# One decoder step in fp32 on one core: the RWKV stage in units of one chunk and eight heads, with two attention stages moved ahead of it

## The chip, the cores and the metric

The kernel runs on one core of a Trainium2 chip. The metric is the device time of one execution in microseconds; the time of a kernel is the median of its runs. TensorE (PE, with its weight loads PEld), VectorE (DVE), ScalarE (ACT), GpSimd (POOL) and SyncE (SP, which issues most of the DMAs) each work through their own instructions in the order in which the program was written out, and wait for each other by semaphores.

## What is computed

One layer over 1024 prompt tokens and 8 sample tokens, d_model 2048, all in fp32. `p = rmsnorm(x) @ w_in` gives the inputs of four branches of width 512 and a gate for each; the gated branches are joined and go through `w_out`. Cut to what matters here:

```python
A  o = softmax-difference attention (4 heads; the samples also over 512 paged cache rows)
B  for each token t, 8 heads of 64:          # RWKV-7, the stage that is changed
     sa = S @ a_t;  S = S * w_t + sa b_t^T + v_t k_t^T;  y_t = S @ r_t
C  Mamba-2 scan (chunks of 128)
X  cross-attention into 256 memory rows (the samples into a cache of their own)
x  = x + concat(A * silu(dg), B * silu(rg), C-branch with its gate mz, X * silu(xg)) @ w_out
```

## The kernel before, in words

**The large products.** `Kern.block` (L554) computes 128 columns of `x @ w` for all 1032 tokens in three groups of 344: for each of four pieces of 512 weight rows, three fp32r matmuls (high by high, high by low, low by high part) per 128 rows and group, 144 in all, at L564. `split_piece` makes the high part on ACT (L540) and the low part on DVE (L541). An object such as `EvShift` (L663, blocks `rs`) or `EvConv` (L689, blocks `mxbc`) evicts each group with ACT and DVE instructions and sends it to DRAM. There are three PSUM banks for these products; the next block's first group takes the bank of the block before it. `ORDER` (L1992) lists the blocks: `dk, dv, dq` of branch A, seven `rs` blocks, four `xq`, six `rs`, `mdt`, eight `mxbc`, four `mz`, and the gates `rg`, `xg`, `dg`. A gate block waits until its branch has its results in DRAM (`ready`, L2007).

**The lanes.** Everything else is written as generators. `Driver.run` (L614) writes out the program: it goes round the lanes, lets one that is due run up to its next `yield d`, and is due again when `K.now`, the planned time, has gone on by `d`; while none is due it writes out `batch` matmuls of the large products, each worth 344/2400 us of planned time. So PE's order is fixed when the kernel is built: bursts of a lane's matmuls between runs of large-product matmuls (`acc` in the profile). `slack` holds a lane back a little unless another lane has just run. If the operands of a burst come late, PE stands still, because the matmuls behind it may not overtake.

**The stages** in `step` (L2074): memory and norms; branch A of the prompt (`mixer_a`); then `Rwkv(K, P).lanes() + [lane_x(K)]`, batch 8; then `lane_dt`; then `lane_m` (`mixer_m`) beside `lane_s` (`samples_a`, then `samples_m`), batch 8; then the output product. `lane_x` is cross-attention of the prompt (`mixer_x`, tiles `xq, xe, xo`) and of the samples (`samples_x`, tiles `sxkp, sxvp`), then `shift_out` and the RWKV step of the samples (`samples_b`, tiles `sst, stt`, DVE instructions over 128x1024). `samples_a` loads 32 cache pages of keys and 32 of values (`sakp, savp`) by indirect DMAs on POOL's queue.

**The RWKV stage.** 16 units; a unit is two of the four 128-row blocks (four of the eight heads) times 128 tokens, that is, two chunks of 64. First eight units for blocks 0 and 1, then eight for blocks 2 and 3, which wait for the last `rs` block. Three lanes: `elements` (L855) loads r, k, v (`rkv`) and forms the scaled operands `ar` and `bk`; `products` (L904) forms the Gram products (`p_gram`), inverts the triangular matrix by five levels of `p_t` (each: DVE mask L979 and 32x32 transposition L983 from `p_t` into `xl`, ACT copy into `rt`, then the matmuls of the next level), `p_w` twice, and then walks the two chunks one after the other with the state S; `norm` (L1078) makes the group norm and writes `ob` out. The walk is:

```python
for c in range(2):                                    # L1035
    z, py = state_products(c) if c else first         # p_z, p_y from S
    if c: yield 0.51
    ... p_sa: 4 matmuls;  copy to sav on DVE and ACT
    yield 0.98
    ... p_s: 4 matmuls, p_y: 4 matmuls;  y copies on ACT;  S = (S + p_s) * pc on DVE
    if c == 0: yield 1.0
```

Each fp32 matmul of a lane is two instructions in the profile, so 4 of them show as x8. `elements` waits for the state of the unit before (`b_s`, L886) before it writes `ar`, of which there is one buffer.

Of the kernel before, what the change touches and what calls it, by code (L numbers as in the profile page):

```python
# [11 lines left out]
F32 = mybir.dt.float32  # L12
# [765 lines left out]
def rwkv_core(K, P, r, k, v, ta, b0, nb, n):  # L778

    nc = K.nc  # L780
# [7 lines left out]
    if n == 128:  # L788
        pn = ps("p_kn")
        for j in range(nb):  # L790
            K.tp(pn[:, j * n:(j + 1) * n], kk[:, j, :], K.id)
        nc.scalar.activation(sq, pn[:, :N].rearrange("p (b t) -> p b t", b=nb), AF.Square)
        rn = P.tile([128, 2, 2 * nb], F32, name="rn", tag="rn")
        nc.vector.tensor_reduce(rn[:, 0, :], sq.rearrange("p b (h t) -> p (b h) t", h=2), axis=AX.X, op=ALU.add)
        nc.vector.tensor_scalar(rn[:, 0, :], rn[:, 0, :], 1e-24, None, op0=ALU.max)
        K.powm(rn[:, 1, :], rn[:, 0, :], 2 * nb)
        rx = P.tile([128, nb * 2, 64], F32, name="rx", tag="pi")
# [3 lines left out]
        for j in range(nb):  # L801
            K.tp(pb[:, j * n:(j + 1) * n], rx[:, 2 * j:2 * j + 2].rearrange("p a b -> p (a b)"), K.id)
# [11 lines left out]
    kn = P.tile([128, nb, n], F32, name="kn", tag="pi" if n == 128 else "kns")  # L814
# [15 lines left out]
class Rwkv:  # L830
# [3 lines left out]
    NB, UNITS = 2, 16  # L834
# [12 lines left out]
    TWO = ("rn", "gst4", "bon128")  # L847
# [7 lines left out]
    def elements(self):  # L855
        K, nc, P, nb = self.K, self.K.nc, self, self.NB
        N, J = nb * 128, nb * 2
        yield from K.wait(f"rs{RS_A[-1]}", 6.0)
        for it in range(self.UNITS):
            b0, t0 = it // 8 * nb, it % 8 * 128  # L860
            if it == 8:
                yield from K.wait(f"rs{RS_B[-1]}", 6.0)
            if it % 2 == 0:
# [5 lines left out]
            rkv = P.tile([128, 3, nb, 128], F32, name="rkv", tag="rkv")  # L869
            for i in range(3):  # L870
                nc.sync.dma_start(out=rkv[:, i], in_=K.sB[4 * i + b0:4 * i + b0 + nb, :, t0:t0 + 128].rearrange(
                    "b p t -> p b t"))
            r, k, v = rkv[:, 0], rkv[:, 1], rkv[:, 2]
            yield 3.5
            if it % 2 == 0:
                ld2, ta2 = rwkv_lora(K, P, lw, b0, nb, 128, 2)
            ld, ta = ld2[:, it % 2], ta2[:, it % 2]
            kk, kn, bon = yield from rwkv_core(K, P, r, k, v, ta, b0, nb, 128)

            ldf = ld.rearrange("p b t -> p (b t)")  # L880
            nc.vector.tensor_tensor_scan(ldf, K.c("reset")[:, :N], ldf, 0.0, op0=ALU.mult, op1=ALU.add)
            cl = ldf.rearrange("p (j t) -> p j t", t=64)
            nc.vector.scalar_tensor_tensor(ta, ta, 1.0, kk, op0=ALU.add, op1=ALU.mult)
            pi = P.tile([128, J, 64], F32, name="pi", tag="pi")
            nc.scalar.activation(pi, cl, AF.Exp, scale=-1.0)
            if it:  # L886
                yield from K.wait(f"b_s{it - 1}")
            j4 = lambda x: x.rearrange("p b (c t) -> p (b c) t", c=2)
            ar = P.tile([128, J, 2, 64], F32, name="ar", tag="ar")
            bk = P.tile([128, J, 2, 64], F32, name="bk", tag="bk")  # L890
            for h in range(2):
                q = slice(h * 64, h * 64 + 64)
                nc.vector.scalar_tensor_tensor(bk[q, :, 1 - h, :], j4(ta)[q], 0.5, pi[q], op0=ALU.mult, op1=ALU.mult)
                nc.vector.tensor_tensor(bk[q, :, h, :], j4(kn)[q], pi[q], op=ALU.mult)
            pe = P.tile([128, J, 65], F32, name="pe", tag="pe")
            nc.gpsimd.memset(pe[:, :, 0:1], 1.0)
            nc.scalar.activation(pe[:, :, 1:65], cl, AF.Exp)
            nc.vector.scalar_tensor_tensor(ar[:, :, 0, :], j4(kk), -1.0, pe[:, :, 0:64], op0=ALU.mult, op1=ALU.mult)
            nc.vector.tensor_tensor(ar[:, :, 1, :], j4(r), pe[:, :, 1:65], op=ALU.mult)
# [1245 lines left out]
```

## Time and profile before

| | |
|---|---|
| runs | 2164.34, 2164.48, 2174.17 us; median 2164.48 |
| profiled execution | 2168.77 us; span 2167.0 us |
| PE / PEld / DVE / ACT / POOL busy | 97% / 91% / 54% / 38% / 9% |
| granted TensorE clock, mean | 0.994 |
| instructions | 41564, of them 16196 matmuls |

A row of a group of instructions gives: line, engine, operation, out<-in, shape, count; busy time in us, mean ns of one; idle time of the engine just before them and what ended it. `whi`, `wlo` are the weight parts, `acc` the large products.

### The profile page before, as it was taken

Reading aid. Unit: us, or ns where it says so; the run is one execution under the profiler, and the core shown is the slowest. Engines: PE = TensorE matmul, PEld = TensorE weight load, DVE = VectorE, ACT = ScalarE, POOL = GpSimd, SP = SyncE. Lnnn points to the kernel's source line nnn. Section 1 sums busy time; section 2 is a strip of 40 time slices with the busy share of each in tenths; the row PEclk is TensorE's granted clock in tenths of the full one; section 3 lists DMA queues with packets and bytes.
Section 4 is the critical chain, followed back from the end, with each engine's and each line's share of the span. In section 5 each row is a group of like instructions: output and inputs, shape, how many; then the busy total and the mean of one; then the engine's idle time right before and its main releaser. Section 6 shows DMA issues by size and latency. Waiting matters only on the chain. (4 is left out here: it accounts for less than half of the span.)

```text
span 2167.0 us, 41564 instructions
## 1 busy us (share of the span) xinstructions
PE 2103.3 (97%) x16196; PEld 1977.2 (91%) x16196; DVE 1169.3 (54%) x2857; ACT 829.6 (38%) x2171; POOL 194.2 (9%) x262
## 2 busy tenths in 40 slices
PE   8999999999999999999999999999999999999997
PEld 6799999999998888888788889999899999999997
DVE  6814353543225567763668885856556254333554
ACT  6724354443223344532444343112121144333544
POOL 2100000000000000020110110620221000000000
PEclk9999999999999999999999999999999999999998
DMA  8643434332322222262323222854666664222791
GB/s 259 192 135 85 133 90 136 84 108 78 91 75 64 59 77 75 69 176 66 94 66 88 65 67 75 256 164 129 174 187 162 203 206 120 70 72 73 235 252 53
DMA packets 320845, 263.45 MB, mean 122 GB/s; under 512 B 29356, under 2 KB 294906, under 8 KB 319952
## 3 DMA queue, kind: packets, MB, share of 16 engines
q1 hardware_dynamic: 307792, 218.97, 35.9%
q0 software_dynamic: 12192, 40.28, 6.3%
q8 instruction: 128, 2.10, 0.4%
q10 hardware_dynamic: 664, 1.54, 0.2%
q14 instruction: 69, 0.57, 0.1%
HBM read 205.98 MB, written 54.80 MB: 120 GB/s over the span
## 5 line engine op out<-in xcount | busy, mean ns | idle before, releaser
L564 PE MATMUL acc<-hh,whi 128*128 128x344 f32 x3312 | 1073.8, 324 | 9.8 <-ACT haB L682 3.2
L564 PE MATMUL acc<-hh,wlo 128*128 128x344 f32 x3312 | 1075.1, 325 | 0.8 <-DVE wlo L541 0.3
L564 PE MATMUL acc<-hl,whi 128*128 128x344 f32 x3312 | 1075.1, 325 | 0.0
L564 PEld LDWEIGHTS acc<-hh,whi 128*128 128x128 f32 x3312 | 624.2, 188 | 18.2 <-ACT whi L540 4.0
L564 PEld LDWEIGHTS acc<-hl,whi 128*128 128x128 f32 x3312 | 625.7, 189 | 4.5 <-issue 1.0
L564 PEld LDWEIGHTS acc<-hh,wlo 128*128 128x128 f32 x3312 | 622.8, 188 | 7.0 <-DVE wlo L541 2.1
L541 DVE TENSOR_TENSOR wlo<-raw,whi 128x512 fp32r<-128x512 f32 x300 | 206.8, 689 | 419.1 <-ACT whi L540 407.3
L540 ACT CAST whi<-raw 128x512 fp32r<-128x512 f32 x300 | 185.3, 618 | 494.3 <-PE acc L564 423.6
L186 PEld LDWEIGHTS p_t<-rt,xl 64*64 64x64 f32 x1280 | 44.8, 134 | 33.9 <-issue 24.0
L186 PE MATMUL p_t<-rt,xl 64*64 64x64 f32 (+1 forms) x1280 | 55.0, 223 | 15.3 <-DVE xl L937 7.6
L1855 ACT ACTIVATE p_out<-xo 128x128 f32<-128x128 f32 (+1 forms) x144 | 39.8, 277 | 77.7 <-DVE xo L1854 73.3
L1534 DVE CUSTOM_DVE_ANT_0 ae<-p_s,al 128x512 f32<-128x512 f32 (+3 forms) x96 | 49.6, 553 | 32.6 <-PE p_s L1531 32.6
L1854 DVE TENSOR_TENSOR xo<-xo,p_out 128x128 f32<-128x128 f32 (+1 forms) x144 | 39.4, 280 | 26.4 <-PE p_out L190 26.1
L1541 ACT ACTIVATE ae<-ae,am 128x128 f32<-128x128 f32 (+7 forms) x64 | 49.2, 771 | 10.4 <-DVE am L1538 10.3
L541 DVE TENSOR_TENSOR wlo<-oraw,whi 128x512 fp32r<-128x512 f32 x48 | 33.2, 692 | 31.7 <-ACT whi L540 31.5
L216 POOL TENSOR_TENSOR osr<-osr,mhalf 128x1 f32<-128x1 f32 (+1 forms) x9 | 6.0, 690 | 453.1 <-DMA xo<-in_x_prompt 328.9
L1531 PE MATMUL p_s<-akm,aqt 128*128 128x512 f32 (+3 forms) x192 | 45.3, 360 | 0.0
L216 POOL TENSOR_TENSOR ass<-ass,mhalf 128x8 f32<-128x8 f32 x4 | 6.6, 1642 | 423.1 <-DVE ass L1582 423.1
L1857 DVE TENSOR_TENSOR xo<-xo,fgc 128x128 f32<-128x128 f32 (+1 forms) x96 | 27.0, 288 | 28.7 <-ACT p_out L1855 27.7
L986 ACT COPY rt<-p_t 128x256 f32<-128x256 f32 x64 | 22.0, 344 | 53.2 <-DVE xl L979 48.7
L715 DVE SCALAR_TENSOR_TENSOR evc<-evx,der,evc 128x344 f32<-128x344 f32 (+1 forms) x72 | 40.5, 567 | 3.1 <-ACT evc L713 2.9
L540 ACT CAST whi<-oraw 128x512 fp32r<-128x512 f32 x48 | 29.6, 617 | 32.5 <-PE acc L564 31.2
(466 smaller groups left out, 2617.8 us busy)
## 6 DMA issues: line engine op xcount, KB each, us to landing
raw<-in_w_in SPq DMA_DIRECT2D x220, 256.0 KB
raw<-in_w_out SPq DMA_DIRECT2D x80, 256.0 KB
oraw<-in_w_out SPq DMA_DIRECT2D x12, 1024.0 KB
evm<-sm SPq DMA_DIRECT2D x48, 172.0 KB
sB<-evs SPq DMA_DIRECT2D x39, 172.0 KB
sA<-evp SPq DMA_DIRECT2D x36, 172.0 KB
evo<-so SPq DMA_DIRECT2D x36, 172.0 KB
sm<-evo SPq DMA_DIRECT2D x36, 172.0 KB
```

What stands on the lines that cost most here:

```text
L186: self.nc.tensor.matmul(out, lhsT=lhsT, rhs=rhs, start=start, stop=stop, **k)
L540: nc.scalar.copy(hi, raw)
L541: nc.vector.tensor_tensor(lo, raw, hi.bitcast(F32), op=ALU.subtract)
L564: nc.tensor.matmul(acc[g][:, :G], lhsT=x[:, k, :], rhs=y, start=kp == ko[0] and k == 0 and x is hi and y is a, stop=kp == ko[-1] and k == ...
L715: nc.vector.scalar_tensor_tensor(e[:, :n], x[:, t:t + n], w(t), e[:, :n], op0=ALU.mult, op1=ALU.add)
L986: nc.scalar.copy(rt[:, :n].rearrange("p a j t -> p (a j t)"), pt[:, :n * J * 32])
L1531: nc.tensor.matmul(p[:, :k1 - k0], lhsT=qt[:, a, c], rhs=km[:, c, k0:k1], start=a == 0, stop=a == 1)
L1534: nc.vector.tensor_tensor_reduce(e[:, c, k0:k1], p[:, :k1 - k0], al[:, x0:x0 + k1 - k0], 1.0, -3e38, ALU.add, ALU.max, m[:, c, pc:pc + 1])
L1541: nc.scalar.activation(e[:, c, :nk], e[:, c, :nk], AF.Exp, bias=m[:, c, 0:1], accum_out=z[:, c:c + 1])
L1854: nc.vector.tensor_tensor(xt, xt, q[:n, k * 128:k * 128 + 128], op=ALU.add)
L1855: nc.scalar.activation(q[:n, k * 128:k * 128 + 128], xt, AF.Square, accum_out=self.ss[:n, 3 * g + k, cb:cb + 1])
L1857: nc.vector.tensor_tensor(xt, xt, self.fg(cb)[:n], op=ALU.mult)
```

## The change

- `Rwkv`: a unit is all four blocks (eight heads) times one chunk of 64 tokens; 16 units. There is no loop over `c`: `p_z`, `p_sa`, `p_s`, `p_y` each come once a unit with eight matmuls. The transpositions of v and `bk` come ahead of the Gram products; two buffers for `ar`, and the last decay of the chunk is copied to `pc` by POOL, so that `elements` waits for `b_n` of two units before instead of `b_s`. The three loads of `rkv` and the store of `ob` move rows of 64 tokens (256 B) instead of 128 (512 B). The lora products are eight of 128 columns instead of four of 256 in every second unit.
- `lane_x` (cross-attention and `samples_x`) and `samples_a` get a `Driver.run` of their own, ahead of the RWKV stage, and the constants `cst1` are loaded for it once more. What was the rest of `lane_x` is `lane_b`. `lane_s` keeps `samples_m`.
- `ORDER`: `xq` ahead of all `rs`; gates in the order `xg, dg, rg`; `KO_OUT` follows.
- `batch` 8 becomes 4 in the RWKV stage, and the turns of `products` get other lengths; `samples_b` goes in four parts with instructions of 128x512. PSUM rings of some tiles change.

```diff
-    NB, UNITS = 2, 16
+    NB, UNITS, N = 4, 16, 256
-    TWO = ("rn", "gst4", "bon128")
+    TWO = ("rn", "gst4", "bon64", "ar", "pc")
     def elements(self):
-        yield from K.wait(f"rs{RS_A[-1]}", 6.0)
+        yield from K.wait(f"rs{RS[-1]}", 6.0)
...
-                nc.sync.dma_start(out=rkv[:, i], in_=K.sB[4 * i + b0:4 * i + b0 + nb, :, t0:t0 + 128].rearrange(
-                    "b p t -> p b t"))
+                nc.sync.dma_start(out=rkv[:, i], in_=K.sB[4 * i:4 * i + 4, :, t0:t0 + 64].rearrange("b p t -> p b t"))
...
+            if it > 1:
+                yield from K.wait(f"b_n{it - 2}")
...
-            if it:
-                yield from K.wait(f"b_s{it - 1}")
...
     def products(self):
+            p = K.ps("p_v", 1)
...
-            yield 2.3
+            yield 3.2
...
-                yield 1.2
+                yield 1.6
...
+            nc.scalar.copy(flat(z), pz[:, :N])
             yield 1.2
...
+            yield 1.0
+            pz = ps("p_sa")
+            for b, h, q, w, n in bh:
+                K.mm(pz[q, n], lhsT=tq[q, b, :], rhs=z[q, b, :], start=True, stop=True)
...
-            for c in range(2):
-                z, py = state_products(c) if c else first
...
+            yield 1.2
+            pz = ps("p_s")
+            for b, h, q, w, n in bh:
+                K.mm(pz[q, n], lhsT=bt[:, b, h, :], rhs=sav[:, b, h, :], start=True, stop=True)
+            for b, h, q, w, n in bh:
+                K.mm(py[q, n], lhsT=gs[:, h, b, 64:128], rhs=sav[:, b, h, :], start=False, stop=b == nb - 1)
+            nc.vector.tensor_tensor(S, S, pz[:, :N].rearrange("p (b t) -> p b t", b=nb), op=ALU.add)
+            nc.vector.tensor_tensor(S, S, bc(pc, 64), op=ALU.mult)
...
 def samples_b
-    for hv in range(2):
-        s = P.tile([128, 16, 64], F32, name="sst", tag="sst")
+    for hv in range(4):
+        s = P.tile([128, 8, 64], F32, name="sst", tag="sst")
...
-RS_A, RS_B = (12, 0, 1, 4, 5, 8, 9), (2, 3, 6, 7, 10, 11)
-ORDER = ([(n, j) for j in range(4) for n in ("dk", "dv", "dq")] + [("rs", j) for j in RS_A] + [("xq", j) for j in range(4)] +
-         [("rs", j) for j in RS_B] + [("mdt", 0)] + [("mxbc", j) for j in range(8)] + [("mz", j) for j in range(4)] +
-         [(n, j) for n in ("rg", "xg", "dg") for j in range(4)])
+RS = (12, 0, 1, 2, 3, 4, 5, 6, 7, 8, 9, 10, 11)
+ORDER = ([(n, j) for j in range(4) for n in ("dk", "dv", "dq")] + [("xq", j) for j in range(4)] + [("rs", j) for j in RS] +
+         [("mdt", 0)] + [("mxbc", j) for j in range(8)] + [("mz", j) for j in range(4)] +
+         [(n, j) for n in ("xg", "dg", "rg") for j in range(4)])
-KO_OUT = [1, 2, 3, 0]
+KO_OUT = [3, 0, 2, 1]
...
 def step
+    with pool("cst") as P:
+        K.cst[1] = P.tile([128, CST[1].shape[1]], F32, name="cst1", tag="cst1")
+        nc.sync.dma_start(out=K.cst[1], in_=I["cst1"])
+        D.run([lane_x(K), lane_sa(K)], batch=8)
     with pool("bp") as P:
-        D.run(Rwkv(K, P).lanes() + [lane_x(K)], batch=8, slack=SLACK)
+        D.run(Rwkv(K, P).lanes() + [lane_b(K)], batch=4, slack=SLACK)
```

## Rows read from the trace of the kernel before

**Rows 1.** The page, parts 1 and 2: PE's busy time, and the span in 40 slices (busy tenths of PE and DVE).
```profile
PE 2103.3 (97%) x16196; PEld 1977.2 (91%) x16196; DVE 1169.3 (54%) x2857; ACT 829.6 (38%) x2171; POOL 194.2 (9%) x262
...
PE   8999999999999999999999999999999999999997
...
DVE  6814353543225567763668885856556254333554
```

**Rows 2.** The stretches of the stages: us from the span's start, length, busy time and count of each engine, granted clock, share of the DMA engines, GB/s. 100 to 647 is branch A; 647 to 1335 the RWKV stage (758 to 909 with cross-attention beside it, 909 to 1027 its wait for the last `rs` block, with `samples_x`); 1441 to 1655 `mixer_m`.
```profile
100.00:647.00 547.00, 546.90 (x3590) 537.48 (x3589) 213.93 (x568) 210.68 (x514) 8.22 (x8) 1.00 0.37 102
647.00:758.00 111.00, 110.83 (x1179) 98.11 (x1177) 62.53 (x166) 38.19 (x106) 6.63 (x11) 1.00 0.22 60
758.00:909.00 151.00, 144.76 (x1527) 123.68 (x1526) 107.37 (x295) 74.69 (x228) 10.19 (x16) 1.00 0.27 75
909.00:1027.00 118.00, 113.91 (x862) 103.92 (x860) 60.66 (x142) 33.71 (x92) 14.43 (x26) 0.97 0.42 118
1027.00:1335.00 308.00, 294.82 (x3220) 256.32 (x3220) 231.20 (x608) 136.69 (x393) 35.31 (x59) 1.00 0.27 73
1335.00:1441.00 106.00, 102.07 (x645) 100.67 (x644) 67.42 (x125) 19.66 (x39) 51.08 (x43) 0.98 0.71 205
```

**Rows 3.** PE's instructions in order of time in a quiet part of the RWKV stage: start us, us, what, count.
```profile
751.45 0.32 PE L564 MATMUL acc<-hh,wlo 128*128 128x344 f32 x1
751.70 0.45 PE L186 MATMUL p_sa<-z,tq 64*64 64x64 f32 x8
752.08 0.43 PE L564 MATMUL acc<-hh,whi 128*128 128x344 f32 x1
752.34 0.32 PE L564 MATMUL acc<-hl,whi 128*128 128x344 f32 x1
752.50 0.32 PE L564 MATMUL acc<-hh,wlo 128*128 128x344 f32 x1
...
753.27 0.32 PE L564 MATMUL acc<-hl,whi 128*128 128x344 f32 x1
753.52 0.45 PE L186 MATMUL p_s<-sav,bt 128*64 128x64 f32 x8
753.80 0.40 PE L186 MATMUL p_y<-sav,gs 128*64 128x64 f32 x8
754.14 0.42 PE L564 MATMUL acc<-hh,wlo 128*128 128x344 f32 x1
754.40 0.32 PE L564 MATMUL acc<-hh,whi 128*128 128x344 f32 x1
```

**Rows 4.** What PE waited for from 647 to 1335, longest in total first: us in total, times, longest.
```profile
PE p_t L186 <- DVE xl L937: 7.6, 9, 1.6
PE p_t L186 <- DVE xl L983: 6.9, 8, 1.4
PE acc L564 <- ACT haB L682: 3.2, 1, 3.2
```

**Rows 5.** The start of two units that follow each other, in PE's order of time.
```profile
721.69 1.16 PE L186 MATMUL p_gram<-ar,bk 64*128 64x128 f32 x16
...
758.10 1.16 PE L186 MATMUL p_gram<-ar,bk 64*128 64x128 f32 x16
```

**Rows 6.** Single units of the RWKV stage, columns as in the stretches of the stages.
```profile
685.00:721.00 36.00, 36.00 (x389) 31.58 (x388) 21.59 (x57) 14.17 (x39) 2.41 (x4) 1.00 0.25 67
1135.00:1174.00 39.00, 36.85 (x409) 32.70 (x408) 30.69 (x100) 19.32 (x62) 3.93 (x7) 1.00 0.28 70
1217.00:1255.00 38.00, 35.94 (x378) 30.34 (x377) 33.85 (x79) 16.01 (x47) 5.22 (x7) 1.00 0.29 79
1255.00:1293.00 38.00, 36.14 (x386) 31.68 (x384) 29.18 (x82) 16.46 (x49) 3.42 (x6) 1.00 0.22 58
```

**Rows 7.** Groups of DVE instructions from 1135 to 1255 (about three units).
```profile
L715 DVE SCALAR_TENSOR_TENSOR evc<-evx,der,evc 128x344 f32<-128x344 f32 (+1 forms) x29 | 16.3, 569 | 0.6 <-ACT evc L713 0.5
L1199 DVE TENSOR_TENSOR stt<-svv,svec 128x1024 f32<-128x1024 f32 x2 | 2.5, 1226 | 0.0
L1064 DVE TENSOR_TENSOR S<-S,pe 128x128 f32<-128x128 f32 x6 | 1.7, 288 | 0.1
L1062 DVE TENSOR_TENSOR S<-S,p_s 128x128 f32<-128x128 f32 x6 | 1.7, 286 | 2.2 <-PE p_s L186 2.2
L961 DVE COPY z<-p_z 128x128 f32<-128x128 f32 x6 | 1.7, 284 | 0.4 <-PE p_z L186 0.2
```

**Rows 8.** Two stops of the large products, in PE's order of time: start us, us, what, and in brackets the idle time before it and what ended it.
```profile
971.96 0.66 PE L564 MATMUL acc<-hh,whi 128*128 128x344 f32 x1 [3.24 <-ACT haB L682]
...
1381.02 0.65 PE L564 MATMUL acc<-hh,whi 128*128 128x344 f32 x1 [3.13 <-DVE evh L734]
```

**Rows 9.** What PE waited for from 1335 to 1655, two of the longest.
```profile
PE p_cv L190 <- ACT mo L1384: 3.6, 1, 3.6
...
PE p_my L190 <- DVE my L1371: 3.0, 5, 0.9
```

**Rows 10.** The tile `rkv` (an instruction that waited for its load: us in total, times).
```profile
  DMA rkv<-sB: 14.5, 8
```

**Rows 11.** The page, part 3: the queue of SP over the whole span (packets, MB, share of the time of 16 DMA engines).
```profile
q1 hardware_dynamic: 307792, 218.97, 35.9%
```

**Rows 12.** The last gate blocks: ACT's instruction on them, first and last start.
```profile
L750 ACT ACTIVATE evg<-acc x36: 437/456/463, 1453.7 to 1772.6; 128x344 f32<-128x344 f32 x36
```

More of the change, by code (lines that the diff above doesn't have):

```diff
@@ L951, in state_products @@
-            def state_products(c):
-                pz, py = ps("p_z"), ps("p_y")
-                for b, h, q, w, n in bh:
-                    K.mm(pz[w, n], lhsT=ar[q, 2 * b + c, 0, :], rhs=S[q, b0 + b, :], start=b == 0, stop=False)
-                for b, h, q, w, n in bh:
-                    K.mm(pz[w, n], lhsT=gs[q, h, 2 * b + c, 0:64], rhs=sav[q, 2 * b + c, h, :], start=False, stop=b == nb - 1)
-                for b, h, q, w, n in bh:
-                    K.mm(py[q, n], lhsT=ar[q, 2 * b + c, 1, :], rhs=S[q, b0 + b, :], start=b == 0, stop=False)
-                z = P.tile([128, nb, 64], F32, name="z", tag="z")
-                nc.vector.tensor_copy(out=z.rearrange("p b t -> p (b t)"), in_=pz[:, :nb * 64])
-                return z, py
@@ L993, in products @@
-                yield 1.2
-                for j in range(J):
-                    for h in range(2):
-                        q = slice(h * 64, h * 64 + 64)
-                        K.mm(ptv[q, :n, j, :], lhsT=lt[q, j, :], rhs=rt[q, :n, j, :], start=False, stop=j == J - 1,
-                             skip_group_check=True)
-            first = state_products(0)
-            tm = P.tile([128, J, 32], F32, name="tm", tag="tm")
-            nc.vector.transpose(flat(tm), pt[:, :J * 32])
-            tq = P.tile([128, J, 64], F32, name="tq", tag="tq")
+                rt = P.tile([128, 2, nb, 32], F32, name="rt", tag="rt")
@@ new lines, in products @@
+                m = 2 if l < 3 else 1
+                nc.scalar.copy(rt[:, :m].rearrange("p a j t -> p (a j t)"), pt[:, :m * nb * 32])
+                yield 1.6
+                for b, h, q, w, n in bh:
+                    K.mm(ptv[q, :m, b, :], lhsT=lt[q, b, :], rhs=rt[q, :m, b, :], start=False, stop=b == nb - 1,
+                         skip_group_check=True)
+            pz, py = ps("p_z"), ps("p_y")
+            for b, h, q, w, n in bh:
+                K.mm(pz[w, n], lhsT=ar[q, b, 0, :], rhs=S[q, b, :], start=b == 0, stop=False)
@@ L1018, in products @@
             yield 1.05
-            for j in range(J):
+            for j in range(nb):
                 for h in range(0, 128, 64):
@@ L1067, in products @@
+            nc.vector.tensor_tensor(S, S, bc(pc, 64), op=ALU.mult)
+            for h in range(2):
+                pyv = py[h * 64:h * 64 + 64, :N].rearrange("p (u w t) -> p u w t", u=2, w=2)
+                for w in range(2):
+                    nc.scalar.copy(y[w * 64:w * 64 + 64, :, h, :], pyv[:, :, w, :])
             self.u[it] = (y, bon)
@@ L1594, in mixer_a, with value_columns @@
     K.mark("a")
-def value_columns(K, P, po, o, half, **slot):
+def value_columns(K, P, po, o, half, ring, **slot):
     nc = K.nc
```

283 lines of the change are left out of this document (130 added, 153 removed).

## The prediction

> **What bounds the kernel now.** I read the page first: PE is busy for 2103.3 of 2167.0 us and its slices show no hole between the first and the last, while DVE swings between 2 and 8 tenths [rows 1]. PE never runs out of large products, so the time is the sum of what PE does plus 63.7 us in which it stands still. Next the stretches of the stages [rows 2]: branch A leaves PE 0.1 us idle in 547, but the RWKV stage has 110.83 + 144.76 + 113.91 + 294.82 = 664.3 us of work in 688, 23.7 us idle, over a third of all idle time. Third, PE in order of time [rows 3]: large-product matmuls start 0.16 us apart, but one lane burst costs more than its matmuls, because PE goes into and out of 64-row shapes. Last, whom PE waits for in that stage: the DVE transpositions ahead of `p_t`, 7.6 and 6.9 us [rows 4]. Those are the two prices of this change: how often PE changes over, and how late DVE is.
>
> The profiled execution took 2168.8 us (span 2167.0 and 1.8 around it), 4.3 above the median of 2164.5. I make the sum against 2168.8 and take 4.3 off at the end.
>
> **What is the same.** The matmuls of a unit keep their number and columns: twice as many heads, half as many chunks. The lora products keep their columns. Nothing in the large products changes. Moved lanes take all their instructions along: `mixer_x`, `samples_x` and `samples_a` need 16 + 32 + 64 loads on SP's and POOL's queues, which now stand ahead of the RWKV loads instead of beside or behind them. SP's extra load of `cst1` has nothing waiting for it but `samples_a`'s page addresses, behind a planned turn of 6 us: nothing, and without that cover some hundred packets at 0.04 us over 16 engines [rows 11], under 1 us. The copy `pc` goes to POOL, 9% busy, and the copy of `z` to ACT, 38% busy [rows 1]: nothing, or 0.3 us a unit if `p_sa` should come before it. The other PSUM rings and the order of the gates and of `KO_OUT` change only which bank or piece comes first: nothing while large products lie between. So PE's work is the same, and only changes of shape and waits count.
>
> **Fewer bursts: -16 us.** Around a `p_sa` of 8, the large products start at 751.45, 752.08, 752.34 [rows 3]: 0.89 us for what is two steps, 0.32, without it; the burst costs 0.57. Around `p_s` and `p_y` together, 16 instructions, they start at 753.27, 754.14, 754.40: 1.13 - 0.32 = 0.81. Eight more instructions add 0.24, so 0.57 - 0.24 = 0.33 is the price of a burst as such. A unit has 13 bursts of `products` before (Gram, five levels, `p_w` twice, and `p_sa`, `p_s/p_y`, `p_z/p_y`, `p_sa`, `p_s/p_y` behind) and 10 after, each of the last ones with twice the matmuls: 3 x 0.33 x 16 units = 16 us. Bounds: nothing, if the longer bursts cost the whole sum, and 3 x 0.57 x 16 = 27. I take the middle one, the only one that has both rows in it.
>
> **Waits in the RWKV stage: +6.5 us.** Of the 23.7 us, 3.2 is one stop of the large products [rows 4]; some 19.5 belong to the lanes. By part [rows 2]: 0.2 in three units with nothing beside them (DVE 62.53 of 111, 56%); 6.2 in the four units beside cross-attention; 13.2 in the eight units beside `mxbc` evictions and `samples_b` (DVE 231.2 of 308, 75%), 1.65 a unit.
> After, no unit runs beside cross-attention, so 6.2 go. But a unit gets shorter. Now it takes 758.10 - 721.69 = 36.4 us [rows 5]. Its planned turns add up to about 20 us of large products before and 16 after, since the second walk goes and `elements` no longer waits for `b_s`; with the bursts I estimate 30 us. A turn also ends sooner: it lasts to the end of a batch, so 1.2 was two batches of 8 x 344/2400, 2.29 planned us or 16 matmuls, and 1.6 is three of 4, 1.72 or 12, in which mask and transposition must be done for the next `p_t`. DVE's work in it hardly falls: of its five small state and copy instructions of 0.28 us [rows 7] three go (`z` and one pair on S), and they get twice as wide, so about 1 us less. Sixteen units of 30 us then hold all the `mxbc` evictions (`evc`, 0.57 us each [rows 7]) in some 11 units, where DVE's 231.2 / 8 = 28.9 us a unit become about 28 in 30. The fullest unit now has DVE busy 33.85 of 38 (89%) and loses 2.1 us; 1135 to 1174 at 79% also loses 2.1, and 685 to 721 at 60% loses none [rows 6]. Waits therefore grow with DVE's share, but not steeply. I take 2.0 us for 11 units and 0.8 for five, 26 us against 19.5. Bounds: 16 x 0.8 = 13 (-6.5), if the halved `samples_b` instructions (1.2 us each before [rows 7]) and the longer turns do away with most; and 16 x 3.0 = 48 (+28), if DVE cannot go past 89%, so that 28 us need 31.5.
>
> **The moved stages: -3 us.** The two stops of the large products are 3.24 and 3.13 us [rows 8], both behind the DVE loops of `samples_x` and `samples_a`; the granted clock of these stretches is 0.97 and 0.98 [rows 2], the mean over a full 2.4 GHz and a spell at 1.2 GHz behind each stop, which is 118 x 0.03 + 106 x 0.02 = 5.7 us more. In the new stage both loops run beside `rs` evictions, which pass through ACT, DVE and ACT again. I keep two such stops: 0, with bounds of -12 (none) and +12 (four). `mixer_m` loses `samples_a`'s POOL queue from beside it, so part of the 3.0 before `p_my` goes; the 3.6 before `p_cv` stays [rows 9]: -3, between -5 and +3 (`samples_m` now comes beside its first chunks).
>
> **Sum.** -16 + 6.5 - 3 = -12.5; 2168.8 - 12.5 - 4.3 = **2152 us**.
>
> **A rule against it.** The unit's loads now have rows of 256 B. The row shows DVE already waiting 14.5 us, in 8 units, for `rkv` [rows 10]. The plan hides the longer transfer: the first use of `rkv` now stands behind `b_n` of two units before, later than the 3.5 us it had. The Trainium skill (DMA: Bandwidth & Descriptors, Specifications) says that transfers under 512 B are below line rate. No row here has the price, and by that sentence these loads would be late.
>
> **Rivals.**
> (a) *No change, 0.30.* The waits eat the bursts' gain: at (19.5 + 16 + 3) / 16 = 2.4 us a unit the sum is zero, 2164. For it: 2.1 is what full units lose already [rows 6]. Against it: six units have little beside them.
> (b) *DVE becomes the bound of the RWKV stage, 0.21; slower.* Place: `p_t`, whose mask and transposition queue on DVE behind `evc` and `elements`, while the turns are now cut to fit a unit of 30 us. PE may not overtake, so what DVE is late PE loses. It decides from 3.1 us a unit on (2.4 and 10.8 / 16). At 3.7, 59 us against 19.5, the sum is +39.5 - 16 - 3 = +20.5: 2185. For it: 93% would be asked of DVE, and 89% is the most that a unit shows. Against it: the fullest unit loses no more than one at 79% [rows 6].
> (c) *Late loads, 0.04; slower.* The unit's loads go from 768 to 1536 packets. SP's queue took 35.9% of 16 x 2167 us for 307792 packets [rows 11], 0.040 us each, so 768 more over 16 engines are 1.9 us a unit; if all of it came on DVE's queue and through to PE, +31: 2183. The skill's sentence above speaks for this one.
> (d) *The end runs dry, 0.05.* The RWKV stage now starts behind all `rs` blocks and cross-attention, by my estimate near 925 instead of 647. With units of 38 us as now it would end near 1533 instead of 1335, and `mixer_m`, 214 us [rows 2] and some 15 more, near 1762, where the gate blocks end as well [rows 12]: the margin of about 100 us is gone, and every further us a unit costs 16. At 38 it just cancels the gain: 2165. At 30 it is nothing.
> The forecast itself has 0.40.
>
> **How the numbers follow.** A difference of 0.5% (10.8 us) is about what a measurement here can tell. The forecast's own range is 2130 (bursts -22, waits 18 in place of 26 and so -1.5, one stop fewer -6, `mixer_m` -5: -34.5) to 2160, most of it below 2153.7, the point of 0.5%; with what (a) has below that I put 0.44 on faster. Same takes most of (a), the upper edge of the forecast and half of (d), 0.31; slower (b) and (c), 0.25. The range, 2130 to 2188, takes in that lower edge, (b) and (c); the bounds of all terms at once lie outside it.
>
> **What would show it.** Right: one burst of `p_sa` x16 a unit, under 0.9 us long; 29 to 32 us between Gram products; 25 to 30 us of PE idle in the RWKV stage, most of it before `p_t`, waiting for `xl`; at most two stops over 3 us; no hole behind the last gate block. Wrong: PE waiting over 45 us for DVE `xl` (b), DVE `kk` waiting for `rkv` in all units (c), idle PE behind the gates (d), or one burst of double width costing as much as two.

## The result, and the profile after

The changed kernel takes 2182.10 us (median of 6 runs, 2175.93 to 2185.56) against 2166.18 for the kernel before in the same session (6 runs): a ratio of 1.0065 (of the means), 95% interval [1.0044, 1.0085]. It is slower by 0.65%, where 2152, a gain, was forecast. Its profiled execution took 2181.65 us, span 2179.9, 12.9 more than the span of before.

The page of the changed kernel, parts 1 and 2 (answers to [rows 1]):

```profile
PE 2098.2 (96%) x16260; PEld 1986.2 (91%) x16260; DVE 1151.5 (53%) x2795; ACT 842.1 (39%) x2231; POOL 199.0 (9%) x286
...
PE   8999999999999899999999999998999999999997
...
DVE  6714353543843422268877776647755254333554
```

PE is busy for 5.1 us less than before and stands still for 2179.9 - 2098.2 = 81.7 us, 18.0 more than the 63.7 before. So the change did take work off PE, and lost more than that in standing still. The slice that fell to 8 near 735 us (the 14th) is the first place to look; the other one (the 28th, near 1500) is the start of `mixer_m`.

The stretches of the changed kernel's stages, columns as in [rows 2]: 543 to 840 is cross-attention beside `samples_a` (and most `rs` evictions), then the RWKV stage waits for the last `rs` block (0.03 us idle from 840 to 940); 940 to 1458 the RWKV stage, 1475 to 1705 `mixer_m` beside `samples_m`, 1705 to 1790 the last gates and the start of the output product.

```profile
543.00:840.00 297.00, 285.19 (x2022) 273.07 (x2021) 133.82 (x286) 77.67 (x204) 89.39 (x96) 0.98 0.57 171
940.00:1458.00 518.00, 489.01 (x5760) 435.74 (x5759) 381.47 (x1001) 237.91 (x710) 53.41 (x99) 1.00 0.24 61
1475.00:1705.00 230.00, 221.61 (x1445) 216.26 (x1445) 145.39 (x219) 46.67 (x90) 14.93 (x25) 0.99 0.51 143
1705.00:1790.00 85.00, 79.10 (x471) 78.15 (x470) 33.58 (x66) 27.15 (x57) 0.00 (x0) 0.94 0.77 228
```

`mixer_m` of before and its last gates, for comparison, with 8.9 and 0.4 us idle and the full clock:

```profile
1441.00:1655.00 214.00, 205.06 (x1548) 196.47 (x1547) 122.09 (x208) 42.40 (x85) 35.02 (x40) 1.00 0.57 159
1655.00:1776.00 121.00, 120.59 (x765) 119.88 (x765) 59.16 (x100) 32.90 (x67) 5.93 (x9) 1.00 0.69 200
```

The reader is to see three things. The RWKV stage stands still for 29.0 us, against 23.7 before [rows 2], and 3.2 of these 23.7 were the stop behind `samples_x` [rows 8]. The new stage of the attentions stands still for 11.8 us, where that stop and `samples_a` in its old place lost 3.2 and 3.9 (1335 to 1441, [rows 2]), and the last gates for 5.9 in place of 0.4. And the granted clock is below 1.00 in three of these stretches: length times what is missing gives 5.9 (attentions) + 2.3 (`mixer_m`) + 5.1 (last gates) = 13.3 us after, against 5.7 in the two stretches of [rows 2].

**The ledger.** Idle +18.0; clock some +7.6 (by the mean clocks of the two spans, 0.991 and 0.994, it would be +6.6). PE's busy time of -5.1 contains that clock, so its work at full clock fell by some 12.7. The table puts this under the terms of the prediction. The stop behind `samples_x` stood among its moved stages, so the waits of the RWKV stage go from 23.7 - 3.2 = 20.5 to 29.0.

| step of the prediction | predicted | measured |
|---|---|---|
| fewer bursts | -16 | -12.7 (what is left of the ledger) |
| waits in the RWKV stage | +6.5 | +8.5 |
| the moved stages (attentions and `mixer_m`) | -3 | +6.6 (idle 4.1, clock 2.5) |
| the last gates | nothing | +10.6 (idle 5.5, clock 5.1) |
| sum against the profiled execution of before | -12.5 | +12.9 (-0.1 elsewhere) |

**The bursts.** PE's instructions of the changed kernel in order of time, around a `p_sa` and around `p_s` and `p_y` (answers to [rows 3]):

```profile
1004.81 0.32 PE L564 MATMUL acc<-hh,whi 128*128 128x344 f32 x1
1005.06 0.68 PE L186 MATMUL p_sa<-z,tq 64*64 64x64 f32 x16
1005.67 0.42 PE L564 MATMUL acc<-hl,whi 128*128 128x344 f32 x1
1005.93 0.31 PE L564 MATMUL acc<-hh,wlo 128*128 128x344 f32 x1
...
1167.60 0.32 PE L564 MATMUL acc<-hl,whi 128*128 128x344 f32 x1
1167.85 0.69 PE L186 MATMUL p_s<-sav,bt 128*64 128x64 f32 x16
1168.36 0.64 PE L186 MATMUL p_y<-sav,gs 128*64 128x64 f32 x16
1168.93 0.43 PE L564 MATMUL acc<-hh,wlo 128*128 128x344 f32 x1
1169.20 0.32 PE L564 MATMUL acc<-hh,whi 128*128 128x344 f32 x1
```

Read as in the prediction, `p_sa` of 16 costs 1005.93 - 1004.81 - 0.32 = 0.80, where two of 8 cost 2 x 0.57; `p_s` with `p_y` of 32 costs 1.60 - 0.32 = 1.28, where two cost 2 x 0.81. Each saves 0.34. The price of a burst as such, 0.33, was right. Their number was not quite: PE's order of time in the RWKV stage has 202 bursts with a tile of `products` before and 162 after, so 40 went and not 48, and 40 x 0.33 = 13.2 is near the 12.7.

**The units and their waits.** The first and the last Gram product (answers to [rows 5]), then what PE waited for from 940 to 1458 (answers to [rows 4]), then how often an instruction waited for the unit's loads over the span (answers to [rows 10]):

```profile
946.12 1.16 PE L186 MATMUL p_gram<-ar,bk 64*128 64x128 f32 x16
...
1413.96 1.16 PE L186 MATMUL p_gram<-ar,bk 64*128 64x128 f32 x16
```

```profile
PE p_t L186 <- DVE xl L953: 13.2, 13, 2.0
PE p_t L186 <- DVE xl L975: 3.1, 5, 1.1
```

```profile
  DMA rkv<-sB: 6.8, 2
```

A unit takes (1413.96 - 946.12) / 15 = 31.2 us; 30 was estimated. The waits stand before `p_t` on `xl`, above all before the first `p_t` of a unit, in 13 of 16 units. DVE waits for `rkv` twice, 6.8 us in all, not eight times and 14.5: the loads of 256 B rows are not later than the old ones were. The Trainium skill (DMA: Bandwidth & Descriptors, Specifications) puts transfers under 512 B below line rate. The profile's page counts 62204 packets under 512 B, but no run here shows their rate.

**The stops.** What PE waited for from 543 to 840, and from 1475 to 1790, in the changed kernel (answers to [rows 8, 9]):

```profile
PE p_vc L190 <- ACT vce L1576: 6.3, 1, 6.3
PE p_xt L190 <- DVE xe L1719: 3.1, 1, 3.1
```

```profile
PE p_mg L190 <- DMA mxg<-sg: 3.8, 1, 3.8
PE acc L564 <- DVE evg L751: 3.3, 2, 3.0
PE acc L564 <- ACT hh L383: 2.8, 1, 2.8
```

These rows name the engine that came last, not the cause. The longest one is followed back in the changed kernel's instructions of all engines, in order of time; brackets hold the idle time before an instruction:

```profile
729.13 0.94 POOL L1617 DMA_INDIRECT savp<-in_cache_diff_v,sapt  x1 [0.30 <-issue]
...
730.07 1.17 POOL L1759 DMA_DIRECT2D sxkp<-in_cache_mem_k  x2
...
735.68 0.69 DVE L1764 TENSOR_TENSOR sxkp<-sxkp,sxqb 128x512 f32<-128x512 f32 x1 [3.48 <-DMA sxkp<-in_cache_mem_k]
...
738.81 0.57 DVE L678 SCALAR_TENSOR_TENSOR evs<-acc,pt,evs 128x343 f32<-128x343 f32 x1
...
739.41 0.16 ACT L682 COPY haB<-acc 128x1 f32<-128x1 f32 x1 [7.71 <-DVE evs L678]
...
741.74 0.59 ACT L1576 COPY vce<-p_sao 128x512 f32<-128x512 f32 x1
...
742.38 0.47 PE L190 MATMUL p_vc<-cst,vce 128*128 128x128 f32 x1 [6.28 <-ACT vce L1576]
```

POOL issues the page loads of `samples_a`, about 1 us each, ahead of the key loads of `samples_x`. DVE stands 3.48 us before a key tile, with the `rs` eviction behind it in its queue; ACT stands 7.71 us before `haB`, which that eviction must free, with the copy `vce` behind it; and PE stands 6.28 before `p_vc`, which needs `vce`. DVE is over half idle in this stage (133.82 of 297 us), but its instructions keep their order: after the wait it works off key tiles for some 3 us before the eviction gets its turn. The stop costs more than its length (the changed kernel, columns as above):

```profile
735.80:742.00 6.20, 0.30 (x2) 0.02 (x1) 6.17 (x12) 0.93 (x4) 1.91 (x4) 0.80 0.73 236
742.00:745.50 3.50, 3.12 (x12) 3.12 (x13) 0.99 (x3) 1.30 (x3) 2.62 (x3) 0.50 0.95 257
745.50:750.00 4.50, 4.50 (x28) 4.50 (x27) 4.47 (x10) 0.17 (x1) 2.64 (x4) 0.91 0.93 308
```

PE works again from 742 at a granted clock of 0.50, the 1.2 GHz level: 3.5 x 0.50 + 4.5 x 0.09 = 2.2 us more, by these rows.

The stop before `p_mg` is SP's queue (its instructions in order of time): four stores of `samples_m` hold it for 7 us, of which the last one waits 5.6 us for a weight load (third row, what SP waited for from 1474 to 1498), and `mxg`, for which PE waits, comes behind.

```profile
1482.46 7.09 SPq L1400 DMA_DIRECT2D srM<-smr  x4
...
1493.13 0.59 SPq L1299 DMA_DIRECT2D mxg<-sg  x1
...
SPq L1400 <- DMA raw<-in_w_in: 5.6, 1, 5.6
```

At the last gates DVE waits for a gate's load `evo`, while the residual loads of `x` (`xo`) fill the DMA engines (share 1.03 in the stretch ahead of it). The second stop there, 2.8 us before `hh`, is not followed back here.

```profile
1731.82 0.52 DVE L752 SCALAR_TENSOR_TENSOR evo<-evg,evo 128x344 f32<-128x344 f32 x1 [6.67 <-DMA evo<-so]
```

```profile
1712.00:1729.00 17.00, 17.00 (x109) 17.00 (x108) 1.99 (x4) 2.77 (x5) 0.00 (x0) 1.00 1.03 284
```

### The profile page after: what moved, and what is told of

The parts are those of the page before. It is cut to its first block, busy times and chain, and to the rows that moved or that the text cites. A ratio compares the mean times of both kernels' runs of the same rounds, so it can differ in the third digit from the quotient of the medians.

```text
span 2179.9 us, 41685 instructions
## 1 busy us (share of the span) xinstructions
PE 2098.2 (96%) x16260; PEld 1986.2 (91%) x16260; DVE 1151.5 (53%) x2795; ACT 842.1 (39%) x2231; POOL 199.0 (9%) x286
## 2 busy tenths in 40 slices
DMA packets 336925, 263.12 MB, mean 121 GB/s; under 512 B 62204, under 2 KB 310986, under 8 KB 336032
## 5 line engine op out<-in xcount | busy, mean ns | idle before, releaser
L186 PEld LDWEIGHTS p_t<-rt,xl 64*64 64x64 f32 x1280 | 44.7, 135 | 41.3 <-issue 24.6
L186 PE MATMUL p_t<-rt,xl 64*64 64x64 f32 (+1 forms) x1280 | 54.3, 223 | 23.4 <-DVE xl L953 13.2
L1617 POOL DMA_INDIRECT savp<-in_cache_diff_v,sapt x32 | 34.3, 1072 | 106.5 <-PE p_sao L186 97.3
L540 ACT CAST whi<-oraw 128x512 fp32r<-128x512 f32 x48 | 29.6, 617 | 32.6 <-PE acc L564 31.2
```

The lines of the kernel that those rows point to most:

```text
L186: self.nc.tensor.matmul(out, lhsT=lhsT, rhs=rhs, start=start, stop=stop, **k)
L540: nc.scalar.copy(hi, raw)
L1617: nc.gpsimd.indirect_dma_start(out=dst, out_offset=None, in_=I[src].rearrange("a p c -> (a p) c"), in_offset=bass.IndirectOffsetOnAxis(ap= ...
```

## Experiments

Four theories stand in the expectations. M: the loss lies in stops of the moved stages; the units gain. U: the units lose, the moves are neutral. E: the RWKV stage ends later, and what follows it runs into the last gates. D: the stop at the last gates is made by full DMA engines. The kernel before takes 2166.2, 2166.2, 2178.5, 2167.3 and 2166.8 us in the sessions of these runs, so each kernel's ratio to before in its own session is compared; the change stands at 1.0065.

### One mend at a time

**m3_x_after_sa**

```diff
     K.mark("x")
+    yield from K.wait("sa")
     with pool("sxp") as P:
```

> The changed kernel with samples_x waiting for the end of samples_a. Theory M: the 6.3 us stop before p_vc, with 6.8 us at half clock behind it (3.4 lost), comes from the key loads of samples_x queued on POOL behind the page loads of samples_a; it goes, 2171 to 2175. Rival: DVE waits for those loads wherever samples_x stands, and the same stop comes later: 2179 to 2185.

Measured 2172.97 us, 1.0027 [1.0015, 1.0039], that is -8 us against the change. What PE waited for from 543 to 945 in it begins with

```profile
PE p_xt L190 <- DVE xe L1719: 3.1, 1, 3.1
```

and `p_vc` is gone from the list. The edit takes all of `samples_x` from beside `samples_a`, its DVE loop as well as its loads, so it shows that the two together made the stop; that POOL's order of loads began it rests on the rows above.

**m4_sm_pool** (in `samples_m`; the same for `xv`, `sc` and `bcv`)

```diff
-            nc.sync.dma_start(out=K.srM[:, g, :, i, :], ...
+            nc.gpsimd.dma_start(out=K.srM[:, g, :, i, :], ...
-        yield 2.0 if k else 8.0
+        yield 2.0 if k else 14.0
+        if k == 0: dx = ...            # was ahead of the loop
```

> The changed kernel with samples_m's small loads and its srM stores on POOL's queue in place of SP's, and its first DVE instruction behind a turn of 14. Theory M: the 3.8 us stop before p_mg at 1492, with 3.4 us at half clock behind it (1.7 lost), comes from mxg queued on SP behind them; it goes, 2175 to 2178. Rival: DVE's wide samples_m instructions stop the same chunk instead: 2180 to 2185.

Measured 2176.90 us, 1.0046 [1.0034, 1.0058], -4 us, with an interval that overlaps the change's. SP now issues `mxg` at 1484.49 in place of 1493.13, and `p_mg` no longer waits. The longer turn for DVE came with the other queue, so neither is shown by itself.

**r3_two** (the edits of m3 and m4 together)

> The changed kernel with only the two mends that paid alone: samples_x behind samples_a (m3, 1.0027 of before) and samples_m's small transfers on POOL's queue (m4, 1.0046); the change itself is at 1.0065. If the stops are costs of their own, the two add: 1.0005 to 1.0015, and what n1_stops lost came from starting cross-attention later. If stops that are mended at one place come back later in any case: 1.003 or more.

Measured 2168.95 us, 1.0007 [0.9996, 1.0018]: the two add (-8 and -4 give -12, -12.6 measured). Two mends that touch no unit take back all of the loss against before that can be measured; the gain that was forecast doesn't come with it. Its profile also shows that not all of it came from the stops. The stages of the attentions and of RWKV in it (the change, from 543 to 945 and to 1458, stands still for 11.8 and 29.0 us):

```profile
543.00:951.00 408.00, 401.40 (x2805) 383.07 (x2804) 166.47 (x363) 109.96 (x283) 93.25 (x106) 1.00 0.49 145
951.00:1461.00 510.00, 486.61 (x5741) 432.67 (x5741) 378.93 (x995) 234.85 (x705) 55.20 (x100) 1.00 0.25 63
```

Idle time falls by 5.2 us in the first and by 5.6 in the second, whose units start 6 us later and were not edited; m3 alone has the same 23.4 there. Why the units wait less is open. The last gates stand still for 2.1 us more.

**m2_gates_old**

```diff
-         [(n, j) for n in ("xg", "dg", "rg") for j in range(4)])
+         [(n, j) for n in ("rg", "xg", "dg") for j in range(4)])
-KO_OUT = [3, 0, 2, 1]
+KO_OUT = [1, 2, 3, 0]
```

> The changed kernel with the gates in their old order (rg, xg, dg) and the old KO_OUT. If the order of the gates makes the two stops behind evg and hh at the last gate blocks (3.0 and 2.8 us, with half clock behind each, 10.6 us in all by the stretches), it takes 2171 to 2173. If they come from where the residual and evm loads fall beside the last gates, whatever their order, it stays at 2178 to 2186 with stops there of the same kind.

Measured 2183.31 us, 1.0070 [1.0057, 1.0083]. The time agrees with the second case, but not its reason: the stops at the last gates do fall, from 5.8 to 1.5 us of PE waiting for `evg` and `hh`, and `mixer_m`, now beside the `rg` gates, stands still for 13.0 us in place of 8.4. The order moves the stops; it is not their cause.

### The parts by themselves

**m1_moves**

```diff
-    NB, UNITS, N = 4, 16, 256      # and all of class Rwkv
+    NB, UNITS = 2, 16              # as before
-        D.run(Rwkv(K, P).lanes() + [lane_b(K)], batch=4, slack=SLACK)
+        D.run(Rwkv(K, P).lanes() + [lane_b(K)], batch=8, slack=SLACK)
```

> The units of before (two blocks of heads, two chunks, batch 8) with everything else of the change: cross-attention and the samples' attention ahead, gates in the new order. Theory M (the changed kernel's loss lies in stops of the moved stages, the units themselves gain): before + 23 of stops and half clock - 6 of waits that stood beside cross-attention, some 2183 (2177 to 2192), and slower than before by 0.5 to 1.2%. Theory U (the moves are neutral, and the new units lose in waits or loads what they gain in bursts, and more): within 5 us of before, 2161 to 2171.

Measured 2205.59 us, 1.0168 [1.0154, 1.0182]. U is refuted in that the moves are not neutral with the old units, and M was too small. Two of the longest waits of PE from 1555 to 1830 in it:

```profile
PE p_sm L190 <- DMA smg<-sg: 11.4, 1, 11.4
PE acc L564 <- ACT whi L540: 10.4, 1, 10.4
```

At 37.5 us a unit the last Gram product comes at 1514, `mixer_m` ends at 1799, behind the last gate at 1772, and PE has nothing left to do beside it. This is rival (d) of the prediction: these moves can't be had with units this long. The other half, the new units without the moves, was not run, so what they gain by themselves rests on the ledger.

**n4_sa_back**

```diff
-        D.run([lane_x(K), lane_sa(K)], batch=8)
+        D.run([lane_x(K)], batch=8)         # samples_a again ahead of samples_m in lane_s
```

> The changed kernel with samples_a back in front of samples_m; cross-attention stays ahead of the RWKV stage. Theory M: the stretch from 543 to 840 loses its stops, -13 to -16; but samples_a now stands beside mixer_m (before it stood beside the mz blocks, ahead of it), and its DVE loop and the later end of samples_m cost 5 to 20 there: 2170 to 2190. If it comes out under 2168, moving samples_a was itself the loss.

Measured 2250.22 us, 1.0389 [1.0370, 1.0407], far over both cases. The first stretch does lose its stops (`p_vc`, `p_xt`), but the end does not bear it: PE waits 32.1 us for `evg` and 14.8 before `p_my`. With the other stages where the change puts them, `samples_a` had to go ahead; m3 shows that how it was put beside `samples_x` was part of the loss.

**n3_batch8** (only `batch=8` again in the RWKV stage)

> The changed kernel with batch 8 in the RWKV stage as before (a turn of 1.6 becomes 16 matmuls in place of 12). If the finer turns are what makes the units wait, the waits of 29 us in the stage fall by 15 or more and the time goes to some 2165. Theory M with the margin at the end: the waits fall, but a unit takes some 35 us, the stage ends 60 us later, mixer_m runs past the last gate blocks, and PE runs dry there: 2178 to 2200.

Measured 2188.81 us, 1.0107 [1.0091, 1.0123]. A unit takes 33.5 us, the wait for the first `xl` falls from 13.2 to 8.9, and PE then waits 10.2 before `p_sm` and 9.8 for `whi` at the end. The finer turns are no cost on balance: with them the stage is shorter by 35 us and the kernel by 9.

**p4_split** (turns between the loops over `p_z`, `p_y` and between `p_s` and `p_y`)

```diff
+            yield 0.3
             for b, h, q, w, n in bh:
                 K.mm(pz[w, n], lhsT=gs[q, h, b, 0:64], ...
```

> The changed kernel with three bursts of a unit cut in two by turns of 0.3 (four matmuls of the large products): between the parts of p_z, between p_z and p_y, between p_s and p_y; the same matmuls. If a burst costs 0.33 us as such, PE's lane time in the stage grows by 3 x 0.33 x 16 = 16 us, and the time by that and what a 2.7 us longer unit costs at the end: 2196 to 2212. If a burst costs no more than its matmuls: 2180 to 2190.

Measured 2207.01 us, 1.0145 [1.0124, 1.0165], +17 us, inside the first case. It can't be split cleanly into burst and end: the stage has 199 bursts in place of 162, a unit takes 33.9 us, PE stands still for 21.4 us in the stage in place of 29.0, and what follows starts later. By the ledger (span +23.8, idle +6.5, mean clock 0.986 in place of 0.991, some 11) some 6 us are left for 37 bursts, half of 37 x 0.33. The price of a burst rests on the rows above and is not confirmed here.

### The end

**p3_late30**

```diff
 def lane_dt(K, P, P2):
+    yield 30.0
```

> The changed kernel with a turn of 30 us of large products ahead of lane_dt, and nothing else: mixer_m ends 30 us later, 50 us ahead of the last gate block in place of 80. Rival E (what the margin at the end has lost shows as stops at the gates): +8 to +25, 2190 to 2207, nearly all of it behind 1700. If the margin is no cost of its own: 2179 to 2185.

Measured 2203.63 us, 1.0133 [1.0113, 1.0153], +15 us for 30 us of lateness with not one instruction added. PE's waits from 1475 to 1830:

```profile
PE acc L564 <- DVE evg L751: 12.7, 3, 7.9
PE p_sm L190 <- DVE smv L1381: 9.3, 1, 9.3
PE acc L564 <- ACT whi L540: 4.6, 1, 4.6
```

E holds at this one delay: half a microsecond for each microsecond that what follows the RWKV stage starts later. That it is a slope is not shown: in p4_split the last Gram product comes 42 us later than in the change, which at 0.5 would cost 21 us, and the whole edit cost 17. Not all of it lies behind 1700, as was expected: `p_sm` at the start of `samples_m` waits 9.3 where it waited 1.2.

**n1_stops** (m3 and m4, and the start of cross-attention moved)

```diff
-    yield from K.wait("xq3", 9.00)
+    yield from K.wait("xq3", 38.00)
```

> The changed kernel with three mends of the moved stages and nothing else: samples_x behind samples_a, cross-attention of the prompt 29 planned us later (so that it no longer begins beside samples_a's DVE loop over the keys), samples_m's small transfers on POOL's queue. RWKV units as in the change. Theory M: -9 and -5 as each alone gave, and -5 for the stop before p_xt (3.1 and 3.4 at half clock) and the small ones beside it: 2161 to 2166, no slower than before. Theory U (what the units lose can't be had back there): the stops turn up elsewhere, over 2172.

Measured 2185.58 us, 1.0085 [1.0067, 1.0103], a miss. r3_two has the other two edits alone and takes 1.0007, so the later start costs 0.8%. It ends the stage of the attentions at 921 (the last `sxvp`; 914 in m3), the last Gram product comes at 1432 (1415 in the change), and behind that PE waits more than in r3_two:

```profile
PE p_my L190 <- DVE my L1346: 6.7, 3, 5.9
PE p_sm L190 <- DVE smv L1381: 5.4, 1, 5.4
```

So lateness can be reached from the front too. It is not the same price as in p3_late30: the last Gram product comes 14 us later than in r3_two, and the kernel loses 17. The RWKV stage has a part in that, since its granted clock from 950 to 1470 is 0.98.

**n2_gram** (n1_stops, and a longer turn behind the Gram products)

```diff
-            yield 3.2
+            yield 4.2
             pt = ps("p_t")
```

> As n1_stops, with the turn behind the Gram products 4.2 in place of 3.2 (seven matmuls of the large products more). PE waits 13.2 us in 13 of 16 units for the first xl of a unit. Theory M: large products fill that wait, a unit is 1 us longer and nothing else: 10 us below n1_stops, 2151 to 2157, faster than before. Rival: DVE is the limit of the unit, the wait moves to the later p_t: within 3 us of n1_stops.

Measured 2178.58 us, 1.0058 [1.0040, 1.0075], 7 us below n1_stops. From 950 to 1470 PE waited

```profile
PE p_t L186 <- DVE xl L975: 9.9, 9, 2.3
PE p_t L186 <- DVE xl L953: 4.0, 6, 1.0
```

so the first wait falls from 11.3 (n1_stops) to 4.0 and comes back at the later levels (2.2 to 9.9): for `xl` the rival is right, 13.5 and 13.9 in all. Other waits in the stage fall, and PE stands still there for 19.4 us in place of 26.5, at a clock of 0.99 in place of 0.98; at the last gates it then waits 14.5 us for `evg` and `whi`. The intervals of the two kernels overlap.

**p1_res and q2_res_slow** (the residual loads on POOL's queue; or on SP's, further apart)

```diff
-                            nc.sync.dma_start(out=xo[g, k][p0:p0 + r, c:c + 1024], ...
+                            nc.gpsimd.dma_start(out=xo[g, k][p0:p0 + r, c:c + 1024], ...
```

```diff
-                        yield 2.00
+                        yield 5.50
```

> The changed kernel with the residual loads of x (12 of some 0.5 MB) on POOL's queue in place of SP's. Theory M: the stop of 3.0 us behind evg at 1729 (with 1.7 lost to half clock) is a gate's evo load that stands behind them in SP's queue; it goes, 2176 to 2179. Rival: the DMA engines are full there anyway and evo comes as late: 2181 to 2185.

> The changed kernel (1.0065 of before) with the residual loads three times as far apart, on SP's queue, and nothing else. Theory D: the stop at 1729 (3.0, and 1.7 at half clock) goes, 1.004 to 1.005 of before. Rival: the loads then reach into the evm loads and the stop at 1778 grows by as much: 1.006 or more.

p1_res: 2188.82 us, 1.0062 [1.0044, 1.0080], no gain, and the stop at the gates grows from 3.0 to some 9 us: POOL issues 8 of the 12 loads within 4.3 us, and from 1710 to 1727 the DMA share is 1.04. Taking the loads off SP's queue did not bring `evo` sooner; that full DMA engines delay it fits these rows, but no run shows it alone. q2_res_slow: 2179.01 us, 1.0054 [1.0040, 1.0069]; the stop at 1729 is gone from its trace and the one on `hh` stays, at 2.4. The time moves the way that D says, but within its interval.

### All mends together

**p2_comb, q1_comb, r1_comb** (m3, m4 with longer turns ahead of `p_sm` and of the first DVE instruction, and the turn of 4.2; residual on POOL's queue, on SP's 5.5 apart, on SP's 3.0 apart; in r1_comb `smx` on POOL's queue too)

> The changed kernel with samples_x behind samples_a, samples_m's small transfers on POOL's queue with longer turns ahead of p_sm and of its DVE work, the residual loads on POOL's queue, and the turn behind the Gram products 4.2. Cross-attention starts as in the change. Theory M: -9, -5, -4, and -8 for the turn: 2154 to 2160, below before. Rival E (the RWKV stage ends later, and what follows it meets the last gate blocks): as with n2_gram the gain is given back behind 1475, over 2170.

> As p2_comb (0.997 of before), but the residual loads back on SP's queue and three times as far apart (turns of 5.5 in place of 2), and a turn of 9 ahead of p_sm. Theory D (the stop at the last gates is a gate's evo load behind residual loads that fill all DMA engines): the 11.4 us stop with its half clock goes, some 12 us, and the 3.9 before p_sm: 0.990 to 0.993 of before. Rival: the last gates stop on evm loads whatever the residual does: 0.996 or more.

> As q1_comb (0.9974 of before) with the residual loads 3.0 apart in place of 5.5, and samples_m's first load (smx) on POOL's queue. Theory D: the 6.3 us stop on evm at the last gates goes since the residual loads end before the evm loads begin, and with it half clock; the 4.4 before p_sm goes since smx no longer waits on SP behind a weight load: 0.991 to 0.994. Rival: the DMA engines are full at the last gates in any spacing, and the stop is on evo or evm again: 0.996 to 0.998.

Measured 0.9969 [0.9957, 0.9981] (2170.25 us, before 2178.48), 0.9974 [0.9963, 0.9984] (2163.62, before 2167.34) and 0.9981 [0.9971, 0.9992] (2161.78, before 2166.80). All three beat both kernels, by 0.2 to 0.3% and by 0.8 to 1% against the change. D's larger hope failed: a stop at the last gates of 6 to 11 us stays in each, on `evo` or on `evm`. From r1_comb:

```profile
1754.00:1763.00 9.00, 0.26 (x1) 0.26 (x2) 8.24 (x18) 8.09 (x19) 0.00 (x0) 0.66 1.06 340
```

PE stands still through this stretch, with the DMA engines full. In these three kernels the spacing of the residual loads only chose which load was late. The wait before `p_sm` falls from 4.1 to 0.4 us with `smx` on POOL's queue (and from 4.7 to 2.5 in r2_comb_gates below, where nothing else differs), so SP's queue made up about half of it or more.

**q3_comb_gates, r2_comb_gates** (q1_comb with the gates and `KO_OUT` as before; the second with `smx` on POOL's queue)

> As q1_comb with the gates in the old order and the old KO_OUT. If the order of the gates is of no account once the stops have other covers: within 0.002 of q1_comb. If rg last is what keeps mixer_m's loads and stores clear of gates: 0.003 or more above q1_comb.

> As q3_comb_gates (0.9995 of before, no stop at the last gates) with samples_m's first load (smx) on POOL's queue. Theory D: the stop of 5.0 before p_sm and its half clock go: 0.996 to 0.997. Rival: DVE, not SP's queue, is late there, 0.999 or more.

Measured 0.9995 [0.9983, 1.0006] and 0.9988 [0.9975, 1.0000]; 0.002 above q1_comb, at the edge of the first case, and between the two cases. No stop of over 0.7 us is left at the last gates; idle time of 6 us in place of their 7 to 9 stands in `mixer_m` and the RWKV stage instead, as in m2_gates_old. How far apart the first residual load and the last gate lie does not settle it: they are some 69 us apart both in before (0.4 us of waiting) and in the change (5.8), 79 in q3_comb_gates (none), but 77 in p1_res (11.1) and 124 in n4_sa_back (24.6).

## Why the prediction was wrong

**Fewer bursts, -16: right in kind and nearly in size.** The price of a burst is 0.34 on both pairs of rows; some -12.7 came of it. The number of bursts was taken from the program, 13 and 10 a unit; in PE's order of time they are 12.6 and 10.1. Before, bursts of two lanes had often met already, and after, the finer turns cut some in two: the `p_sa` at 1102.66 is two matmuls, one of the large products, then fourteen.

**Waits in the RWKV stage, +6.5: near in size, in part by luck.** 29.0 us against 20.5; 25 to 30 were given, most of it before `p_t` on `xl`, and units of 29 to 32 us. Rival (b), DVE as the bound, would have shown 45 us and didn't. But the reason given was DVE's share, 28 in 30 us in 11 units. From Gram product to Gram product DVE is busy for 23.4 of 31.2 us in the mean and for 30.0 of 34.0 at most, and the units late in the stage, at 20 of 30, still lose 1.1 to 1.8 us each where 0.8 was taken. The wait sits at the first level, in the turn behind the Gram products, and the prediction did not say so.

**The moved stages, -3: this step failed,** and with it the term beside it that was put at nothing, the last gates. The first measured +6.6 and the second +10.6, together 20 us of the miss of 25.4 against the profiled execution. "I keep two such stops: 0" took the stops as a property of the DVE loops, to be carried along. In the rows they come from what shares a queue. The prediction counted the moved loads (16 + 32 + 64); it did not go through the queues instruction by instruction: POOL now has the pages of `samples_a` ahead of the keys of `samples_x`, DVE the keys ahead of the `rs` evictions, SP the stores of `samples_m` ahead of `mxg` of the first chunk. m3_x_after_sa and m4_sm_pool each take one of these stops away and gain 8 and 4 us, and r3_two shows that they add to -12.6. That is about what stops and half clock were worth, but in its profile 5.6 us of it are waits of the RWKV stage, which neither edit touched, so the match is in part luck.

**"The order of the gates and of `KO_OUT` ... nothing": right for the order (m2_gates_old), wrong for the place.** The gates lose 5.9 in place of 0.4 idle and 5.1 of clock. The cause of this part stays open. In the rows DVE waits there for `evo` beside full DMA engines, but no edit at the gates alone (m2_gates_old, p1_res, q2_res_slow) changed the time beyond its interval, r3_two keeps stops of 8.0 us there, and where the stops were gone (q3_comb_gates, r2_comb_gates) waits stood elsewhere.

**Rival (d)** was given as a cliff, at units of 38 us, and at 38 as the gain cancelled, 2165. m1_moves shows it where it was put, at 37.5 us a unit, but at +39. p3_late30 shows that lateness costs well before it, 15 us for 30. How far it has a share in the change's own loss at the gates is open: the residual loads begin as far from the last gate as before, 69 us.

**The rule on 256 B rows, rival (c): not borne out.** 6.8 us of waiting in 2 units, where all units were to wait.

**The clock** was priced in the prediction only for the two stops known; six stops over 2 us are now followed by a granted clock of 0.50, and the stretches cost 13.3 us. Who forecasts a new stop has to forecast its clock as well.

## What to carry to other kernels

When a stage is moved beside another, write down for each in-order queue (DMA issue queues too) which instruction that waits for a load now stands ahead of which eviction or operand; here VectorE, 45% busy, and ScalarE, 26%, stopped the chain all the same. Where one engine sets the time, an edit that only lets a chain of lanes end later can be paid for at the end, well before the chain is the last to end: test it by a plain delay. A part of a change that gains can hide behind one that loses: mend or undo the parts one at a time before judging the whole.

## What the runs showed that was not expected

Every stop of PE of over 2 us in the changed kernel, from branch A to the output product, was followed by work at a granted clock of 0.50 (2.04, 2.77, 3.02, 3.06, 3.84 and 6.28 us). The shortest is a wait before `p_t` at 1421, in a stage whose mean rounds to 1.00; the 3.57 us before `p_cv` at 1652 in the kernel before [rows 9] was not followed by it, so length alone does not settle it, and no run here tells what does. The stretches behind these two, of the changed kernel and of before:

```profile
1421.00:1425.00 4.00, 3.88 (x28) 3.61 (x28) 0.87 (x2) 0.37 (x1) 0.00 (x0) 0.64 0.21 61
...
1652.00:1660.00 8.00, 7.98 (x52) 7.84 (x52) 7.48 (x11) 2.23 (x5) 1.06 (x2) 1.00 0.79 214
```

A load on another queue did not get through sooner while the DMA engines were full: with the residual loads on POOL's queue in place of SP's, PE's stop for `evo` became 6 us longer, not shorter (p1_res).
